# One float32 kernel of two transformer blocks: expert weights loaded by 2 MB into double places and by 1 MB into single ones

## The chip, the core and the metric

The kernel runs on one core of a Trainium2 chip. The metric is the device time of one execution in microseconds. Engines are called as the profile calls them: PE (matmuls), DVE (VectorE), ACT (ScalarE), POOL (GpSimd) and SP, whose queue issues most transfers.

## What is computed

Two blocks follow each other on 256 tokens of width 1024, in float32. The first has two layers, each with a gated feed-forward part, a mixer of attention and Fourier branches, and another feed-forward part. The second has one layer: a mixer of block attention and gated linear attention, and a mixture of 32 experts of which every token takes four. Cut to the part that matters here:

```python
logits = tokens @ w_router + b_router
top_logits, top_idx = lax.top_k(logits, 4)
top_w = softmax(top_logits)
def expert(e, rows):                      # the tokens that chose e
    hid = tokens[rows] @ w_exp_in[e] + b_exp_in[e]       # [n, 1024] @ [1024, 2048]
    return clamped_swiglu(hid) @ w_exp_out[e] + b_exp_out[e]   # [n, 1024] @ [1024, 1024]
y = sum over the chosen experts of top_w * expert
out = rmsnorm(x + gate2 * y, final_norm_w)
```

## The kernel before

All weights come as one stream of chunks, class `Stream` (lines 253 to 331). A chunk is one transfer of usually 1 MB, [128, 2048] float32. `load` (line 264) takes the first of a ring of places, `self.raw`, and issues the transfer on SP's queue (line 272). `convert` (line 278) takes half a chunk, a piece, and makes the two parts whose sum is the weight: `wh` on ACT (line 284) and `wl`, the rest, on DVE (line 285). When the second piece of a chunk is converted, its place is free and `load` is called again. `get` (line 319) hands out the next piece to the matmuls; before it does, `fill` converts until five pieces are ahead. In the program's order the conversion is therefore up to five pieces, HL, ahead of the matmuls. All engines work through their instructions in the order in which this Python code emits them, and SP's queue likewise: a load that has to wait for its place holds up the loads behind it.

The ring has three places of its own (RAW). At the end of the second mixer `more` (line 292, called in lines 1260 and 1279) adds four places in tiles of the second mixer that are free by then (pool `p2`, tags `r0` to `r3`), for good, and two in the tiles of the transposed input (`xth`, `xtl`) which serve once.

The expert stage, `moe`, runs over quarters q: `hidden(e, j)` takes a quarter of the first layer of expert e, q = 4 e + j, two chunks of 1 MB, and multiplies it with the slots of the expert's tokens (lines 1536 and 1537, one matmul with `wh` and one with `wl` for each of eight blocks of the contraction). `outputs(e, j)` does the same with a quarter of the second layer, one chunk of 1 MB (lines 1579 and 1580); it runs five quarters behind. So the stream of the stage, written out in the loop ahead of line 390, is: two first-layer chunks of quarter q, then (from q = 5) one second-layer chunk of quarter q - 5. Between them stand the smaller steps: the activation on DVE and ACT (`folded`, lines 1549 to 1565), the copies out of the accumulators (lines 1539 and 1584), the sum over the experts (line 1523), and for each group of four experts the gathering of its tokens (lines 1475 and 1493). `later` defers such a step by a number of pieces.

The loop over q at the end of `moe` also places some steps by hand. At q = 17, 20 and 22 come the transposition of the expert weights and the sum of the second-layer biases (`bias_part`, `bias_sum`, line 1597). At q = 26 the pool `bp`, which holds the biases, is left, and the last two rows, the gate of the residual and the gain of the last norm, each spread over all partitions, are loaded in its place as `fin` on POOL's queue (line 1631). `gated_sum` (lines 1607 and 1608) is the first to use them, after the last expert.

Of the kernel before, what the change touches and what calls it, by code (L numbers as in the profile page):

```python
# [23 lines left out]
OUT_ORDER = [*range(4 * NE - 3), 4 * NE - 2, 4 * NE - 3, 4 * NE - 1]  # L24
GLA_LEVELS = [1, 2, 4, 8, 16, 32, 64]


# ---------------------------------------------------------------- weight stream
# [77 lines left out]
# ---------------------------------------------------------------- constants of the shapes  # L106
# [47 lines left out]
# ---------------------------------------------------------------- data layout on the host  # L154
def cols(v):
    """[..., 128 n] -> [128, ..., n]: a vector as columns of 128."""
    v = np.asarray(v)
    return np.ascontiguousarray(np.moveaxis(v.reshape(*v.shape[:-1], -1, 128), -1, 0))


def layout(a):
    o = {}
    parts = []
    for ch in dense_chunks():
# [5 lines left out]
        a["w_exp_in_2"][0].reshape(NE, 2, 4, 128, 4, 256, 2).transpose(0, 4, 1, 3, 2, 6, 5)  # L170
    ).reshape(NE, 4, 2, 128, 2048)
# [29 lines left out]
# ---------------------------------------------------------------- the program  # L201
def build(tc, I, out):
# [26 lines left out]
    # persistent  # L229
# [22 lines left out]
    # ------------------------------------------------ weight stream  # L252
    class Stream:
        """Weight chunks: loaded whole, split into two exact float32r parts by halves, and given out by halves."""

        def __init__(self, chunks, raw, hl):
            self.ch, self.raw, self.hl = chunks, [(raw, "raw")] * RAW, [hl] * HL
            self.d = self.c = self.u = self.step = 0
            self.R, self.C = {}, {}
            self.pre, self.post = [], []  # L260
            self.side = self.units = None
            self.hold = False

        def load(self, parts=1):
            if self.d < len(self.ch):
                ap, w = self.ch[self.d]
                p, tag = self.raw[0]
                self.raw = self.raw[1:] + self.raw[:1]
                r = p.tile([128, 2048], FT, name="raw", tag=tag)
                for i in range(parts):  # L270
                    sl = slice(w // parts * i, w // parts * (i + 1))
                    SP.dma_start(r[:, sl], ap[:, sl])
                    if parts == 2 and i == 0:
                        load_x(256, 512)
                self.R[self.d] = r
                self.d += 1

        def convert(self):
            i, h = divmod(self.c, 2)
            r, w = self.R[i], self.ch[i][1] // 2  # L280
            p = self.hl[self.c % len(self.hl)]
            hi = p.tile([128, 1024], FR, name="wh")
            lo = p.tile([128, 1024], FR, name="wl")
            A.activation(hi[:, :w], r[:, h * w:h * w + w], AF.Copy)  # L284
            V.tensor_tensor(lo[:, :w], r[:, h * w:h * w + w], hi[:, :w], OP.subtract)  # L285
            self.C[self.c] = (hi, lo)
            self.c += 1
            if h:
                del self.R[i]
                self.load()  # L290

        def more(self, p, tags, once=False):
            """Further places for raw chunks, filled at once and, unless once, again in their turn."""
            for tag in tags:
                self.raw.insert(0, (p, tag))
                self.load()
                if once:
                    self.raw.pop()
# [10 lines left out]
        def start(self):  # L309
            self.load(2)  # L310
            load_x(512, D)
            for _ in range(RAW - 1):
                self.load()

        def fill(self):
            while self.c < min(self.u + len(self.hl), 2 * len(self.ch)):
                self.convert()

        def get(self):
            self.step += 1  # L320
# [4 lines left out]
            if self.u % 2 == 0:  # L325
                if self.units:
                    self.units.step()
# [23 lines left out]
    def mm_tok(ps, X, klist, w, last, mid=None):  # L351
        """ps[t] += X[k]^T W[k] for the k of a chunk; mid comes between the chunk's halves."""
# [11 lines left out]
    def wide(p, X, lo=0, hi=8):  # L364
        """p [128 outputs, 256 tokens] += W[k]^T X[k] for the k of half a chunk."""
# [5 lines left out]
    def rms_power(o, ss, scale, eps):  # L371
        """o = (ss * scale + eps) ** -0.5"""
# [17 lines left out]
    raw = enter("raw", RAW)  # L390
    hl = enter("hl", HL)
    st = Stream(dense, raw, hl)
# [21 lines left out]
    # ---------------------------------------- side work of the first block, a piece per chunk  # L414
# [72 lines left out]
    def make_xt(X, src, half, gcol=None, after=None):  # L487
        """X[k] = (src columns k)^T * gcol for the four k of a half."""
# [17 lines left out]
    def rms_of(ss, eps, name="rstd", pre=None):  # L506
        """(mean + eps) ** -0.5 from the halves' sums of squares, which pre scales first."""
# [8 lines left out]
    class Norm:  # L516
        """The normed, transposed x of the next stage, in two halves of the columns."""
# [18 lines left out]
    # ---------------------------------------- FFN  # L536
# [74 lines left out]
    # ---------------------------------------- units of softmax work, stepped between chunks  # L611
    class Steps:
        """Units under way take one stage per chunk, the oldest first; one new unit starts per chunk."""
# [12 lines left out]
        def finish(self):  # L626
            while self.step():
                pass
            st.units = None

    # ---------------------------------------- first mixer
    def mixer(l, norm, next_gain):
# [16 lines left out]
        # -- Fourier branch between the projections  # L649
# [17 lines left out]
        def row_rstd(dg):  # L667
            """rstd along the free dimension, on every partition"""
# [61 lines left out]
        # -- attention, in steps between the chunks of the values and the gates  # L730
# [53 lines left out]
        def diff_unit(h, qt):  # L784
# [39 lines left out]
            # the heads' norms; their gain comes with the transposition  # L824
# [18 lines left out]
        st.units = att  # L843
# [29 lines left out]
        # -- branch outputs, gated and merged  # L873
# [36 lines left out]
        # -- output projection  # L910
# [881 lines left out]
```

## Time and profile before

| | us |
|---|---|
| three runs, median (lowest to highest) | 2688.63 (2688.14 to 2689.32) |
| profiled execution, its span | 2688.0 |
| PE busy | 2605.0 |
| DVE busy | 2080.7 |
| ACT busy | 1723.2 |

The profiled execution has no time of its own beside its span; the span runs from its first instruction to its last and lies 0.6 us under the median of the runs. Busy times are unions of an engine's instructions over the span. The expert stage takes the part from about 1622 us to the end; what lies before it belongs to the first block and the second mixer. A group of instructions is read as: line, engine, operation, output and inputs, count, busy time, mean duration in ns, idle time of the engine just before them and what ended most of it.

### The profile page before, as it was taken

The page shows a single profiled execution, that of the slowest core. Times are in us where ns is not written, and L with a number is a line of the kernel's source. Part 1 is how long each engine was busy: PE and PEld are TensorE (multiplying, and loading weights), DVE is VectorE, ACT ScalarE, POOL GpSimd, SP SyncE. Part 2 cuts the span into 40 slices and gives each one's busy share as a digit, 9 for nine tenths or more (in the row PEclk, how much of TensorE's full clock was granted, in tenths as well). Part 3 has the DMA queues.
Part 4 walks back from the last instruction along what each step waited for, and adds up shares of the span by engine and source line. Part 5 has one row for each costly group of instructions (what it writes and reads, how often), then busy time and mean ns, then how long its engine had stood idle before and what let it go on. Part 6 is the DMA issues. An engine that isn't in the chain of part 4 may idle for free.

```text
span 2688.0 us, 34842 instructions
## 1 busy us (share of the span) xinstructions
PE 2605.0 (97%) x12700; PEld 2092.6 (78%) x12700; DVE 2080.7 (77%) x2717; ACT 1723.2 (64%) x2290; POOL 182.6 (7%) x255
## 2 busy tenths in 40 slices
PE   8999999999999999999999998999999999999996
PEld 6889888887787978778798886777777777777775
DVE  5656766666666676655656679999999999999997
ACT  5444554444444454544555538989898989888886
POOL 1000000001101000000000102000000000000000
PEclk9999999999999999999999999999999999999999
DMA  7655445655566444565444566999999999999995
GB/s 282 220 216 207 153 149 192 221 218 211 213 225 245 149 153 172 193 226 180 158 149 151 175 246 251 381 399 389 381 393 388 386 388 391 388 393 389 390 395 203
DMA packets 106227, 712.89 MB, mean 265 GB/s; under 512 B 13380, under 2 KB 14052, under 8 KB 25409
## 3 DMA queue, kind: packets, MB, share of 16 engines
q1 hardware_dynamic: 92976, 667.03, 65.9%
q0 software_dynamic: 12928, 43.05, 4.3%
q8 instruction: 101, 1.65, 0.2%
q14 instruction: 78, 0.63, 0.1%
q10 hardware_dynamic: 144, 0.52, 0.0%
HBM read 709.40 MB, written 3.77 MB: 265 GB/s over the span
## 4 chain that ended last, share of the span: by engine, by line
PE 84%; DVE 9%; issue 3%; ACT 3%; DMA 0%; POOL 0%; DVEq 0%; SPq 0%; ACTq 0%; POOLq 0%
PE hid L1536 7%; PE hid L1537 6%; DVE wl L285 6%; PE po L1580 3%; PE pf L1549 3%; PE g L347 3%; PE u L347 3%; PE g L348 3%; PE u L349 3%; PE g L349 3%; PE u L348 3%; PE d L347 3%; PE d L349 3%; PE d L348 3%; PE y L1523 3%
## 5 line engine op out<-in xcount | busy, mean ns | idle before, releaser
L285 DVE TENSOR_TENSOR wl<-raw,wh 128x1024 fp32r<-128x1024 f32 (+2 forms) x1274 | 1504.7, 1218 | 424.7 <-ACT wh L284 414.9
L284 ACT ACTIVATE wh<-raw 128x1024 fp32r<-128x1024 f32 (+2 forms) x1274 | 1294.3, 1050 | 527.7 <-PE d L349 126.5
L1536 PE MATMUL hid<-wh,xgt 128*128 128x512 f32 x1024 | 441.0, 431 | 0.2 <-ACT hs L1539 0.2
L1537 PE MATMUL hid<-wl,xgt 128*128 128x512 f32 x1024 | 404.8, 395 | 0.0
L1580 PE MATMUL po<-wl,act 128*128 128x512 f32 x512 | 208.6, 407 | 32.9 <-DVE wl L285 32.9
L1536 PEld LDWEIGHTS hid<-wh,xgt 128*128 128x128 f32 x1024 | 193.3, 189 | 54.3 <-issue 16.1
L1537 PEld LDWEIGHTS hid<-wl,xgt 128*128 128x128 f32 x1024 | 193.3, 189 | 53.3 <-issue 14.3
L1579 PE MATMUL po<-wh,act 128*128 128x512 f32 x512 | 204.0, 398 | 2.8 <-ACT osb L1584 2.8
L1580 PEld LDWEIGHTS po<-wl,act 128*128 128x128 f32 x512 | 96.1, 188 | 78.5 <-DVE wl L285 57.6
L347 PE MATMUL g<-wh,xth 128*128 128x512 f32 (+1 forms) x384 | 147.0, 383 | 0.0
L347 PE MATMUL u<-wh,xth 128*128 128x512 f32 (+1 forms) x384 | 146.0, 380 | 0.0
L348 PE MATMUL g<-wl,xth 128*128 128x512 f32 (+1 forms) x384 | 144.8, 377 | 0.0
L349 PE MATMUL g<-wh,xtl 128*128 128x512 f32 (+1 forms) x384 | 144.5, 376 | 0.0
L349 PE MATMUL u<-wh,xtl 128*128 128x512 f32 (+1 forms) x384 | 144.4, 376 | 0.0
L348 PE MATMUL u<-wl,xth 128*128 128x512 f32 (+1 forms) x384 | 144.1, 375 | 0.0
L347 PE MATMUL d<-wh,hth 128*128 128x512 f32 x352 | 139.8, 397 | 0.0
L349 PE MATMUL d<-wh,htl 128*128 128x512 f32 x352 | 138.8, 394 | 0.0
L348 PE MATMUL d<-wl,hth 128*128 128x512 f32 x352 | 138.8, 394 | 0.0
L1549 PEld LDWEIGHTS pf<-fold,hs 128*128 128x128 f32 x1024 | 130.8, 192 | 8.8 <-issue 1.3
L1549 PE MATMUL pf<-fold,hs 128*128 128x64 f32 x1024 | 129.1, 269 | 1.4 <-DVE v L1555 0.9
L1523 PE MATMUL y<-osb,ohw 128*128 128x512 f32 x256 | 123.0, 603 | 2.1 <-ACT osb L1584 2.1
L1493 POOL TENSOR_TENSOR wdup<-oh,wgt 128x128 f32<-128x128 f32 x64 | 72.5, 1162 | 741.4 <-PE wts L1500 510.0
(488 smaller groups left out, 4441.6 us busy)
## 6 DMA issues: line engine op xcount, KB each, us to landing
raw<-d_exp_in SPq DMA_DIRECT2D x256, 1024.0 KB, 7.3
raw<-d_dense SPq DMA_DIRECT2D x245, 1024.0 KB, 4.8
raw<-d_exp_out SPq DMA_DIRECT2D x128, 1024.0 KB, 7.5
ada_w<-d_ada POOLq DMA_DIRECT2D x96, 256.0 KB, 4.6
bias<-tables POOLq DMA_DIRECT2D x2, 1920.0 KB, 12.7
bg<-d_b_gate POOLq DMA_DIRECT2D x12, 256.0 KB, 4.2
raw<-d_dense SPq DMA_DIRECT2D x4, 768.0 KB, 4.5
raw<-d_dense SPq DMA_DIRECT2D x5, 512.0 KB, 3.6
```

The costliest lines, as they stand in the source:

```text
L284: A.activation(hi[:, :w], r[:, h * w:h * w + w], AF.Copy)
L285: V.tensor_tensor(lo[:, :w], r[:, h * w:h * w + w], hi[:, :w], OP.subtract)
L347: T.matmul(ps, lhsT=xh, rhs=wh, start=start, stop=False)
L348: T.matmul(ps, lhsT=xh, rhs=wl, start=False, stop=False)
L349: T.matmul(ps, lhsT=xl, rhs=wh, start=False, stop=stop_)
L1493: G.tensor_tensor(d[:, :, c], oh, wg, OP.mult)
L1523: T.matmul(y[t][n], lhsT=grp[e // 4].w[:, e % 4, t], rhs=osb[e, n], start=e == 0, stop=e == NE - 1)
L1536: T.matmul(ph, lhsT=lhs, rhs=wh[:, 512 * i:512 * i + 512], start=k == 0, stop=False)
L1537: T.matmul(ph, lhsT=lhs, rhs=wl[:, 512 * i:512 * i + 512], start=False, stop=k == 7)
L1549: T.matmul(pf[:, 4 * (c // 2) + 2 * (j % 2) + c % 2], lhsT=hs[:, 128 * c:128 * c + 128], rhs=fold, start=True, stop=True)
L1579: T.matmul(po, lhsT=lhs, rhs=wh[:, 512 * i:512 * i + 512], start=k == 0, stop=False)
L1580: T.matmul(po, lhsT=lhs, rhs=wl[:, 512 * i:512 * i + 512], start=False, stop=k == 7)
```

## The change

The first layer of an expert is stored and loaded by quarters of 2 MB, [128, 4096], which are converted in four pieces of the same size as before. The stream has two kinds of places. A double place holds 2 MB, a single one 1 MB. The three own places are one tile now; while dense weights are loaded they are three single places. When no dense chunk is left to load, places 0 and 1, once converted, are held back and become one double place, and place 2 goes on as the only single one. The tiles of `p2` become two double places (`r23`, `r01`), the transposed input's tile one double place that serves once. At q = 14 the pool `bp` is left and a further single place, `hx`, takes its memory. When no first-layer load is left, double places serve as single ones. Of the chunks of both sizes that have a free place, the one that comes first in the stream is loaded first.

The two parts of a piece share a tile, and so do pairs of tiles in the second mixer and of the transposed input. The bias steps come at q = 8, 10 and 12. The last two rows are loaded after the last first-layer quarter, on SP's queue, into a single place. The constants KIND_IN and KIND_OUT set every expert chunk to HALVES, conversion by pieces of 1024 columns; the other two kinds, WHOLE and DIRECT, are not used. Cut to its core:

```diff
+KIND_IN, KIND_OUT = HALVES, (HALVES, HALVES, HALVES, HALVES)
...
-        a["w_exp_in_2"][0].reshape(NE, 2, 4, 128, 4, 256, 2).transpose(0, 4, 1, 3, 2, 6, 5)
-    ).reshape(NE, 4, 2, 128, 2048)
+        a["w_exp_in_2"][0].reshape(NE, 2, 4, 128, 4, 256, 2).transpose(0, 4, 3, 1, 2, 6, 5)
+    ).reshape(NE, 4, 128, 4096)
...
+            self.todo = {w: [i for i, (_, n) in enumerate(chunks) if (n > 2048) == (w > 2048)] for w in (2048, 4096)}
+            self.own = raw.tile([128, 2048 * RAW], FT, name="raw")
+            self.free, self.held = {2048: list(range(RAW)), 4096: []}, []
...
+        def place(self, w):
+            p = self.free[w].pop(0)
+            if isinstance(p, int):
+                return p, self.own[:, 2048 * p:2048 * p + w]
+            pool_, tag = p
+            return p, pool_.tile([128, w], FT, name="raw", tag=tag)
+        def load(self, parts=1, most=1000):
+            for _ in range(most):
+                ready = [w for w in (2048, 4096) if self.free[w] and self.todo[w]]
+                if not ready:
+                    break
+                w = min(ready, key=lambda w: self.todo[w][0])
+                i = self.todo[w].pop(0)
+                self.T[i], r = self.place(w)
...
+                    SP.dma_start(r[:, sl], ap[:, sl])
...
+            if not self.todo[4096]:
+                self.free[2048] += self.free[4096]
+                self.free[4096] = []
+        def done(self, i):
+            del self.R[i]
+            p = self.T.pop(i)
+            if p not in self.once:
+                w = 4096 if self.ch[i][1] > 2048 else 2048
+                if w == 2048 and p in (0, 1) and self.todo[2048] and self.todo[2048][0] >= DENSE:
+                    self.held.append(p)
+                    if len(self.held) == 2:
+                        self.free[4096].append(0)
+                else:
+                    self.free[w].append(p)
+                self.load()
...
+                    both = self.part("w")
+                    hi, lo = both[:, :1024], both[:, 1024:]
...
+        def rows(self, srcs):
+            _, r = self.place(2048)
+            for i, src in enumerate(srcs):
+                SP.dma_start(r[:, 1024 * i:1024 * i + 1024], src)
+            return r[:, :1024], r[:, 1024:]
...
-            dense += [(I["exp_in"][q // 4, q % 4, h], 2048) for h in range(2)]
+            dense.append((I["exp_in"][q // 4, q % 4], 4096))
...
     def new_xt():
-        return (xtp[0].tile([128, 8, S], FR, name="xth"), xtp[0].tile([128, 8, S], FR, name="xtl"))
+        t = xtp[0].tile([128, 2, 8, S], FR, name="xt")
+        return t[:, 0], t[:, 1]
...
-        st.more(p2, ("r2", "r3", "r0", "r1"))
+        st.more(p2, ("r23", "r01"), 4096)
...
-        st.more(xtp[0], ("xth", "xtl"), once=True)
+        st.more(xtp[0], ("xt",), 4096, once=True)
...
-            if q == 17:
+            if q == 8:
                 later(POST, 1, bias_part)
-            if q in (20, 22):
-                later(POST, 1, lambda: bias_sum(q // 2 - 10))
+            if q in (10, 12):
+                later(POST, 1, lambda: bias_sum(q // 2 - 5))
...
-            if q == 26:
+            if q == 14:
                 leave("bp")
-                fp = enter("fin", 1, side="right")
-                for src in (bcast_row(mods, D, 3 * D), bcast_row(I["final_norm"], D)):
-                    fin.append(fp.tile([128, D], FT, name=f"fin{len(fin)}"))
-                    G.dma_start(fin[-1], src)
+                st.more(enter("hx", 1, side="right"), ("hx",), 2048)
+            if q == 4 * NE:
+                fin.extend(st.rows((bcast_row(mods, D, 3 * D), bcast_row(I["final_norm"], D))))
```

## Rows read from the trace of the kernel before

**Rows 1.** The page: the span, and each engine's busy time, share and instructions.

```profile
span 2688.0 us, 34842 instructions
PE 2605.0 (97%) x12700; PEld 2092.6 (78%) x12700; DVE 2080.7 (77%) x2717; ACT 1723.2 (64%) x2290; POOL 182.6 (7%) x255
```

**Rows 2.** Busy times by window, expert stage; last columns: granted clock, DMA share, GB/s.

```profile
1740.00:1900.00 160.00, 156.00 (x715) 118.67 (x715) 158.13 (x180) 142.44 (x179) 10.53 (x10) 1.00 0.99 392
1900.00:2100.00 200.00, 192.91 (x903) 149.38 (x903) 197.13 (x225) 177.83 (x226) 11.18 (x12) 0.99 0.99 386
...
2500.00:2640.00 140.00, 133.61 (x609) 101.11 (x608) 139.32 (x157) 123.90 (x153) 5.78 (x4) 1.00 0.99 394
sum 900.00, PE 868.26 PEld 666.23 DVE 890.74 ACT 802.90 POOL 52.91; mean PE 173.65 PEld 133.25 DVE 178.15 ACT 160.58 POOL 10.58
```

**Rows 3.** Groups by line and shape, window 1760 to 2600 us.

```profile
L285 DVE TENSOR_TENSOR wl<-raw,wh 128x1024 fp32r<-128x1024 f32 x621 | 722.4, 1220 | 5.3 <-ACT wh L284 1.3
L284 ACT ACTIVATE wh<-raw 128x1024 fp32r<-128x1024 f32 x621 | 620.3, 1051 | 7.0 <-PE hid L1536 6.3
...
L1537 PE MATMUL hid<-wl,xgt 128*128 128x512 f32 x828 | 327.1, 395 | 0.0
L1580 PE MATMUL po<-wl,act 128*128 128x512 f32 x416 | 169.7, 408 | 27.5 <-DVE wl L285 27.5
...
L1597 PE MATMUL y<-bo,wgtT 32*128 32x512 f32 x8 | 4.0, 613 | 0.0
```

**Rows 4.** Waits in that window (engine, line, released by: total, times, longest); SP's queue first.

```profile
SPq L272 <- DVE wl L285: 605.4, 253, 4.5
...
POOL fin L1631 <- PE y L1597: 63.8, 1, 63.8
...
DVE wl L285 <- ACT wh L284: 1.3, 3, 0.5
```

**Rows 5.** Transfers in that window: GB/s in 40 slices of 21 us; issues, median to landing.

```profile
GB/s 415 379 418 371 404 387 394 379 361 404 382 389 396 382 377 397 384 399 391 389 368 402 396 386 386 404 376 379 399 394 380 404 373 394 383 401 388 385 396 409
...
raw<-d_exp_in SPq DMA_DIRECT2D x208, 1024.0 KB, 7.3
raw<-d_exp_out SPq DMA_DIRECT2D x103, 1024.0 KB, 7.5
```

**Rows 6.** Line 272's time to landing: 1760 to 2600 us, then 0 to 1560 us (dense).

```profile
DMA to landing us min/median/max: 5.8/7.4/9.1
...
DMA to landing us min/median/max: 3.2/4.8/12.0
```

**Rows 7.** SP's queue in time order, 1695 to 1720 us: start, duration, issue.

```profile
1695.58 2.60 SPq L272 DMA_DIRECT2D raw<-d_exp_in  x2
1700.12 0.33 SPq L272 DMA_DIRECT2D raw<-d_exp_out  x1
1703.99 2.60 SPq L272 DMA_DIRECT2D raw<-d_exp_in  x2
1708.86 0.33 SPq L272 DMA_DIRECT2D raw<-d_exp_out  x1
```

**Rows 8.** DVE in time order, the end of the kernel.

```profile
2650.52 5.76 DVE L285 TENSOR_TENSOR wl<-raw,wh 128x1024 fp32r<-128x1024 f32 x5
...
2664.89 1.22 DVE L285 TENSOR_TENSOR wl<-raw,wh 128x1024 fp32r<-128x1024 f32 x1 [0.28 <-ACT wh L284]
2671.42 0.69 DVE L1607 TENSOR_TENSOR osb<-y,fin 128x512 f32<-128x512 f32 x1 [5.31 <-PE y L1523]
```

**Rows 9.** The transfers of the last two rows: size, median time to landing.

```profile
fin<-mods POOLq DMA_DIRECT2D x1, 512.0 KB, 7.6
fin<-d_final_norm POOLq DMA_DIRECT2D x1, 512.0 KB, 10.7
```

**Rows 10.** Busy times by window around the start of the experts (columns as in Rows 2).

```profile
1620.00:1630.00 10.00, 8.14 (x42) 7.59 (x42) 8.83 (x13) 8.32 (x13) 1.70 (x2) 0.66 0.23 79
1650.00:1660.00 10.00, 8.43 (x48) 6.76 (x48) 9.93 (x14) 9.52 (x14) 8.47 (x7) 1.00 0.43 163
```

More of the change, by code (lines that the diff above doesn't have):

```diff
@@ L260, in __init__, with pieces @@
             self.pre, self.post = [], []
-            self.side = self.units = None
+            self.side = self.steps = None
+            self.T, self.once = {}, set()
             self.hold = False
[L264 to L271, printed above, removed]
+        def pieces(self, i):
+            return 4 if self.ch[i][1] > 2048 else 2
@@ new lines, in place @@
+        def place(self, w):
[12 more added lines that the diff above has]
+                self.T[i], r = self.place(w)
+                ap, n = self.ch[i]
+                for k in range(parts):
+                    sl = slice(n // parts * k, n // parts * (k + 1))
@@ L292, in more @@
[L292 to L298, printed above, removed]
+                self.R[i] = r
+            if not self.todo[4096]:
[13 more added lines that the diff above has]
+                self.load()
@@ new lines, in part @@
+        def part(self, name):
+            p, tag = self.hl.pop(0)
+            self.hl.append((p, tag))
+            return p.tile([128, 2048], FR, name=name, tag=tag)
+        def convert(self):
+            i, h, kind = self.units[self.c]
+            r, w = self.R[i], self.ch[i][1]
+            if kind == DIRECT:
+                self.C[self.c] = (r, None)
+            else:
+                if kind == HALVES:
+                    w //= self.pieces(i)
+                    both = self.part("w")
+                    hi, lo = both[:, :1024], both[:, 1024:]
+                else:
+                    hi, lo = self.part("wh"), self.part("wl")
+                r = r[:, h * w:h * w + w]
+                A.activation(hi[:, :w], r, AF.Copy)
+                V.tensor_tensor(lo[:, :w], r, hi[:, :w], OP.subtract)
+                self.C[self.c] = (hi, lo)
+            self.c += 1
+            if kind == WHOLE or kind == HALVES and h == self.pieces(i) - 1:
+                self.done(i)
@@ L300, in due, with more @@
+        def more(self, p, tags, w, once=False):
+            for tag in tags:
+                if once:
+                    self.once.add((p, tag))
+                self.free[w].insert(0, (p, tag))
+                self.load()
+        def rows(self, srcs):
[3 more added lines that the diff above has]
+            return r[:, :1024], r[:, 1024:]
         def due(self, q):
@@ L309, in start, with parts @@
         def start(self):
-            self.load(2)
+            self.load(2, 1)
             load_x(512, D)
-            for _ in range(RAW - 1):
-                self.load()
+            self.load()
         def fill(self):
-            while self.c < min(self.u + len(self.hl), 2 * len(self.ch)):
+            def parts(n):
+                return {HALVES: 1, WHOLE: 2, DIRECT: 0}[self.units[n][2]]
+            while self.c < len(self.units) and \
+                    sum(parts(n) for n in range(self.u, self.c + 1)) <= len(self.hl):
+                if self.units[self.c][0] not in self.R:
+                    break
                 self.convert()
         def get(self):
-            self.step += 1
+            if self.u and self.units[self.u - 1][2] == DIRECT:
+                self.done(self.units[self.u - 1][0])
+            self.step += 1 if self.units[self.u][2] == HALVES else 2
             self.due(self.pre)
@@ L388, in build @@
             dense.append((I["exp_out"][e, j // 2, j % 2], 2048))
-    raw = enter("raw", RAW)
-    hl = enter("hl", HL)
-    st = Stream(dense, raw, hl)
+    raw = enter("raw", 1)
+    hl = enter("hl", 1)
+    DENSE = len(dense_chunks())
+    kinds = [HALVES] * DENSE
+    for q in range(4 * NE + 5):
+        kinds += [KIND_IN] * (q < 4 * NE)
+        kinds += [KIND_OUT[OUT_ORDER[q - 5] % 4]] * (q >= 5)
+    st = Stream(dense, kinds, raw, hl)
     sm = enter("small", 2)
@@ L628, in finish @@
                 pass
-            st.units = None
+            st.steps = None
     def mixer(l, norm, next_gain):
@@ L1201, in gla_unit @@
             A.activation(junk[:, :256], ob[:, t, vs], AF.Square, accum_out=obs[:, 4 * t + h:4 * t + h + 1])
-        att = st.units = Steps([gla_unit(h, t) for h in range(4) for t in range(2)])
+        att = st.steps = Steps([gla_unit(h, t) for h in range(4) for t in range(2)])
         zb = enter("zb", 2)
@@ L1523, in combine, with weigh @@
             T.matmul(y[t][n], lhsT=grp[e // 4].w[:, e % 4, t], rhs=osb[e, n], start=e == 0, stop=e == NE - 1)
+        unit = {}
+        def weigh(ps, x, k, start, stop_):
+            n = k % 4
+            if n == 0 or n == 2 and unit["kind"] == HALVES:
+                unit["kind"] = st.units[st.u][2]
+                unit["w"] = get()
+            wh, wl = unit["w"]
+            if unit["kind"] == HALVES:
+                n %= 2
+            sl = slice(512 * n, 512 * n + 512)
+            x = x.rearrange("p c s -> p (c s)")
+            if unit["kind"] == DIRECT:
+                T.matmul(ps, lhsT=x.bitcast(FT), rhs=wh[:, sl], start=start, stop=stop_)
+            else:
+                T.matmul(ps, lhsT=x, rhs=wh[:, sl], start=start, stop=False)
+                T.matmul(ps, lhsT=x, rhs=wl[:, sl], start=False, stop=stop_)
         def hidden(e, j):
@@ L1528, in hidden @@
             ph = hbank("hid")
[L1529 to L1537 removed]
+            for k in range(8):
+                if e + j == 0 and k in (2, 4):
+                    grp[0].pair(k + 2)
+                weigh(ph, X[k // 4][:, k % 4, e % 4], k, k == 0, k == 7)
             hs = w2.tile([128, 512], FT, name="hs")
@@ L1573, in outputs @@
             po = pos_[n]
[L1574 to L1580 removed]
+            for k in range(4 * kh, 4 * kh + 4):
+                weigh(po, act[e][:, k], k, k == 0, k == 7)
             if kh:
@@ L1722, in rest @@
                 for h in range(2):
-                    w = weights(I["exp_in"][one, j, h])
+                    w = weights(I["exp_in"][one, j, :, 2048 * h:2048 * h + 2048])
                     for i in range(4):
```

62 lines of the change are left out of this document (20 added, 42 removed).

## The prediction

> **What bounds the kernel now.** The profiled execution has a span of 2688.0 us [rows 1]; the runs shown have a median of 2688.63 us, 0.6 us more, so a sum made against the span is moved over to the median unchanged. I read the page first. PE is busy for 97% of the span and would be named the bound by that figure alone [rows 1]. The change touches the expert stage, so next come the busy times by window over that stage, 1740 to 2640 us [rows 2]: VectorE (DVE) is busy 890.7 of 900 us, PE 868.3, ScalarE (ACT) 802.9, and the DMA engines show a share of 0.99 at 386 to 394 GB/s. Three resources look full, so the waits must decide. The groups of instructions by line say that DVE's subtraction `wl` (line 285) takes 1220 ns and sat idle before it for 5.3 us in 840, while PE waited 27.5 us at line 1580 for exactly that subtraction [rows 3]. The list of waits has no line in which ACT or DVE waits for a weight transfer; the transfers are what waits: SP's queue stood 605.4 us for DVE to free a place [rows 4]. So **DVE sets the pace**, and the stream keeps up with it. How closely it keeps up is the question here.
>
> One quarter of an expert (index q, 128 of them) reads 2 MB of first-layer and 1 MB of second-layer weights. In the stretch of 840 us 208 first-layer transfers were issued, two per quarter [rows 5], so a quarter lasts 840/104 = 8.08 us.
>
> **The change, part by part.**
>
> *Places.* Before, 1 MB transfers go in order round seven places. A transfer is on its way for 7.4 us (5.8 to 9.1) in this stage [rows 6], out of 7 x 2.69 = 18.9 us that a place is held; the data lie ready long before DVE wants them. After, the first layer has three double places (the fourth, in the transposed-input tile, serves once), so the load of quarter q+3 goes out when quarter q has been converted: 24 us for 2 MB, ample. The second layer is different. Places 0 and 1 become the third double place when the dense weights end, so the second layer has **one place**, number 2, until the place `hx` is opened at q = 14. It holds the first second-layer chunk (used at q = 5) from early on. The nine that follow, used at q = 6 to 14, can each be issued only when the chunk before has been converted, and are wanted one quarter later. The tenth goes into `hx`, after which two places give each load a quarter more, and the wait ends.
>
> *What one of the nine costs.* SP issues in order on one queue, and second-layer loads leave 2.3 to 2.6 us after the last first-layer load [rows 7]; after the change the 2 MB load of quarter q+3 stands just ahead. Neither a 2 MB load nor one behind it is in the trace, so I bound it. The best slice moved 418 GB/s [rows 5], 1.049 MB in 2.51 us; a 1 MB transfer without a full queue lands after 4.8 us [rows 6], so 2.3 us are not movement. The last of 3 MB lands 2.3 + 3 x 2.51 = 9.8 us after the issue of the first-layer load. It should be there when DVE has finished the next quarter's first layer, 8.08 us after that issue, less the 1.05 us that ACT's `wh` needs ahead of DVE [rows 3]: 7.0 us. That leaves 2.8 us of stall. But a stall falls after the issue of the next first-layer load, so that load gains what was lost: successive stalls add up to 2.8 us in pairs, **1.4 us per quarter** at the low end. For the high end I take the stage's slowest rate, 386 GB/s [rows 2], hence 2.72 us per MB, and add the spread of landings, 9.1 - 7.4 = 1.7 us, because a late transfer is lost and an early one gives nothing back: 2.3 + 8.15 + 1.7 = 12.2 us, a stall of 5.2 us, 2.6 per quarter. Between them I take **2.0 us**, the middle, as the queue will be emptier than in the rows of before but landings will still scatter. DVE has no slack to make it up later [rows 2]. Nine quarters: 9 x 2.0 = **18 us**, ends 12.6 and 23.4, and 25 if each of the nine lost the whole 2.8.
>
> The Trainium skill (DMA: Bandwidth & Descriptors, Anatomy of one DMA) fits one transfer as about 2.0 us plus its bytes at 436 GB/s, for the software-generated path. By that fit the last of 3 MB would land after 9.2 us, the stall would be 1.1 us per quarter, and the sum about 10 us, where the rows give 12.6 at the least; here the rows decide. The Trainium skill (Trainium Kernel Development and Optimization, Best Practices) asks to double-buffer so that DMA and compute overlap, which speaks against a single place; no row of before shows a stream with one.
>
> *The start.* Nine places are filled before the experts begin, with 9 MB either way: at 1620 to 1630 us the DMA engines move only 79 GB/s, since nothing is free [rows 10]. After the change one of the nine holds a second-layer chunk early, and the first-layer loads behind it have 5 quarters' time. 0 us.
>
> *Longer rows.* A first-layer transfer moves 16 KB per partition instead of 8. No row shows that; the two rates used above, 418 and 386 GB/s, stand for a better and a worse one.
>
> *Steady state from q = 15.* DVE's work is the same six conversions per quarter at the same width, so 8.08 us stays: 0 us, covered by DVE itself. Half as many first-layer issues (128 fewer SP instructions) save nothing, as SP mostly waits [rows 4].
>
> *Joined tiles.* The two parts of a converted piece, of `xt` and of the second mixer's tiles now share a tile, so a writer waits for the last reader of both halves. In `prod` the readers of the two halves end one matmul apart, 0.4 us by the nearest row [rows 3]. For some ten new `xt` tiles that is 0 to 4 us; nothing here removes work, so no gain. I take 0.5 us. In the experts ACT may be released one matmul later, but DVE waited only 1.3 us for ACT [rows 4]: 0.
>
> *The bias steps* move from q = 17 to 22 to q = 8 to 12. They are eight matmuls of about 0.6 us, 4.0 us in all [rows 3], with transposes and one ACT copy; DVE has no part in them. Cost 0 under DVE's work, 4 us if that cover were gone. POOL's queue loses two DMA issues that waited 63.8 us for these matmuls with nobody waiting for them [rows 4]: 0.
>
> *The last rows.* Two transfers of 512 KB move from POOL to the end of SP's queue. They go into `hx` when the chunk four before the last has been converted. Ten conversions belong to the last five chunks. The row at 2650.52 us merges five conversions and six more follow, the last at 2664.89, so the second of the ten is the third of that row and ends at about 2654 us [rows 8]. With the slowest landing of these rows in the busy stage, 10.7 us [rows 9], they are there at 2665, and the first use is at 2671.4 [rows 8]. Cost 0, with 6 us of cover; the bound if it failed is the same 10.7 us.
>
> Sum: 2688.6 + 18 + 0.5 = **2707 us**.
>
> **The rivals.**
>
> *No stall of size (within 0.2%).* If second-layer loads land within about 7.6 us of the first-layer issue, the nine stalls stay under 0.6 us each. For it: in the busy stage a load lands in as little as 5.8 us [rows 6]. Against: that row is for 1 MB, and 2 MB more stand ahead. The time would be about 2691 us.
>
> *DMA is the bound and longer transfers relieve it (faster).* For it: the share of 0.99. Against: nobody waits for a weight. It could at most give back DVE's idle time in the stage, 900 - 890.7 = 9.3 us [rows 2], by way of the gaps before line 285: 2679 us. It decides only if the slowed stretch from q = 6 to 14 costs less than that. The fit on the skill's page named above would have two 1 MB transfers cost 2.0 us more than one of 2 MB. The trace moves a MB every 2.69 us, well under one transfer's time, so fixed parts overlap and are not paid.
>
> *The second place comes late, or a loaded stream stays short with two (much slower).* Every further quarter costs another 2.0 us: ten more give 2727 us, all of them some 2930. For it: `hx` takes memory that other tiles leave. Against: the old `fin` tiles took the same memory, and their load left as soon as the bias matmuls ended [rows 4]. A second form: PE, waiting more, is granted a lower clock, as at 1620 to 1630 us (0.66). But at 1650 to 1660 it was busy only 84% of the time and kept 1.00 [rows 10].
>
> **How the numbers follow.** A measurement of this kernel can tell about 0.2%, 5.4 us, from no change: faster is below 2683.2, slower above 2694.0. The forecast has a chance of 0.76, the first rival 0.13, the second 0.05, the third 0.06. Hence faster 0.05, same 0.13, slower 0.82. The forecast's own ends are 2701 (12.6 us) and 2714 (25 us). The range is 2692 to 2717: down into the first rival's reach, and up by the 3.5 us that the joined tiles may cost beyond what is taken.
>
> **What would show it.** Right: in the changed profile, a stretch of about 75 us near 1660 to 1745 us in which DVE's busy share drops to some 80%, ACT's `wh` waits for transfers into `raw`, and second-layer issues come one per 10 us; after it the pace is 8.08 us again and DVE 99% busy. Half the first-layer issues, each 2 MB. `fin` waits for nobody at the end. Wrong: that stretch is as full as before, DVE idles on throughout the stage, or the time lies under 2694 us.

## The result and the profile after

The changed kernel takes **2710.3 us** (median of four runs, 2708.95 to 2713.3), the kernel before 2688.39 us in four runs of the same comparison. The ratio is 1.0079, with a 95% interval of [1.0066, 1.0092]. The change costs 21.9 us, and the profiled executions show nearly the same: their spans are 2709.0 and 2688.0 us, 21.0 us apart. In the program of after, the two parts of a piece come from ACT in line 335 (`w<-raw`) and from DVE in line 336; every load of the stream is issued in line 295.

The first view is the page: span, busy times, and the expert loads with their size and median time to landing.

```profile
span 2709.0 us, 34061 instructions
PE 2615.1 (97%) x12700; PEld 2096.4 (77%) x12700; DVE 2080.0 (77%) x2717; ACT 1722.5 (64%) x2290; POOL 180.0 (7%) x253
...
raw<-d_exp_in SPq DMA_DIRECT2D x128, 2048.0 KB, 9.5
...
raw<-d_exp_out SPq DMA_DIRECT2D x128, 1024.0 KB, 8.6
```

DVE has done the same work as before: 2080.0 us in 2717 instructions, against 2080.7 [rows 1]. So the 21 us of added span are idle time, and the question is where that lies. The busy times by window over the expert stage answer it (columns as in [rows 2]):

```profile
1660.00:1760.00 100.00, 86.35 (x376) 63.35 (x375) 78.57 (x89) 70.94 (x91) 7.01 (x6) 0.95 0.83 312
1760.00:1860.00 100.00, 96.04 (x450) 73.97 (x450) 98.98 (x114) 88.80 (x114) 2.69 (x4) 1.00 0.98 384
1860.00:2060.00 200.00, 193.06 (x899) 147.93 (x898) 198.24 (x225) 179.22 (x225) 14.26 (x12) 1.00 0.98 390
...
2460.00:2660.00 200.00, 193.22 (x891) 147.73 (x890) 197.51 (x224) 177.81 (x222) 5.80 (x4) 1.00 0.98 387
```

The first of these stretches in the kernel before:

```profile
1660.00:1760.00 100.00, 96.71 (x458) 74.83 (x457) 99.06 (x113) 89.77 (x115) 7.36 (x6) 1.00 0.96 375
```

DVE is busy 78.57 us of the first 100, where it was busy 99.06. That is 20.5 us lost in one stretch. From 1760 us on it is as full as before. Even the DMA engines fell there, from a share of 0.96 at 375 GB/s to 0.83 at 312: they too had nothing to do for part of the time, because the next load had no place. Ahead of the stretch nothing is lost. DVE's step for the second quarter of the experts starts at the same time in both kernels:

```profile
1656.60 0.68 DVE L1643 TENSOR_TENSOR v<-pf,ebias 128x512 f32<-128x512 f32 x1
```

```profile
1656.49 0.69 DVE L1555 TENSOR_TENSOR v<-pf,ebias 128x512 f32<-128x512 f32 x1
```

The first line is of after, the second of before: 0.11 us apart. Now the waits of after, from 1660 to 1780 us (engine and line, what released it: total, times, longest):

```profile
ACT w L335 <- DMA raw<-d_exp_out: 22.3, 9, 4.7
DVE w L336 <- ACT w L335: 21.3, 12, 4.2
...
PE po L1616 <- DVE w L336: 9.4, 10, 1.5
```

**Nine** waits for second-layer transfers, 22.3 us together, 2.5 each. ACT waits for the transfer, DVE for ACT, PE for DVE. No such line is in [rows 4], nor in after from 1780 us on. The single waits stand in ACT's timeline (start, duration, idle time before and its releaser):

```profile
1671.09 2.95 ACT L335 ACTIVATE w<-raw 128x1024 fp32r<-128x1024 f32 x3 [4.66 <-DMA raw<-d_exp_out]
...
1680.90 2.96 ACT L335 ACTIVATE w<-raw 128x1024 fp32r<-128x1024 f32 x3 [0.75 <-DMA raw<-d_exp_out]
...
1691.42 1.06 ACT L335 ACTIVATE w<-raw 128x1024 fp32r<-128x1024 f32 x1 [2.37 <-DMA raw<-d_exp_out]
...
1701.29 3.90 ACT L335 ACTIVATE w<-raw 128x1024 fp32r<-128x1024 f32 x4 [0.79 <-DMA raw<-d_exp_out]
...
1711.73 2.96 ACT L335 ACTIVATE w<-raw 128x1024 fp32r<-128x1024 f32 x3 [3.68 <-DMA raw<-d_exp_out]
...
1721.74 3.90 ACT L335 ACTIVATE w<-raw 128x1024 fp32r<-128x1024 f32 x4 [0.93 <-DMA raw<-d_exp_out]
...
1732.75 2.95 ACT L335 ACTIVATE w<-raw 128x1024 fp32r<-128x1024 f32 x3 [4.25 <-DMA raw<-d_exp_out]
...
1742.65 3.91 ACT L335 ACTIVATE w<-raw 128x1024 fp32r<-128x1024 f32 x4 [1.31 <-DMA raw<-d_exp_out]
...
1753.02 2.95 ACT L335 ACTIVATE w<-raw 128x1024 fp32r<-128x1024 f32 x3 [3.60 <-DMA raw<-d_exp_out]
```

SP's queue in time order, for three of these quarters:

```profile
1681.03 0.33 SPq L295 DMA_DIRECT2D raw<-d_exp_in  x1
1684.72 0.33 SPq L295 DMA_DIRECT2D raw<-d_exp_out  x1
1690.04 0.33 SPq L295 DMA_DIRECT2D raw<-d_exp_in  x1
1696.50 0.33 SPq L295 DMA_DIRECT2D raw<-d_exp_out  x1
1701.37 0.33 SPq L295 DMA_DIRECT2D raw<-d_exp_in  x1
1705.10 0.33 SPq L295 DMA_DIRECT2D raw<-d_exp_out  x1
```

Two kinds of quarter alternate. In the **long** one the second-layer load leaves close behind a 2 MB load (1681.03, then 1684.72) and is there at 1691.42, 10.4 us after the first-layer issue. ACT was ready 2.37 us earlier. In the **short** one the stall before has let the first-layer load go ahead (1690.04), and the second-layer load leaves alone, at 1696.50. It still takes 4.79 us, and ACT was ready at 1701.29 - 0.79 = 1700.50, 4.00 us after the issue. So a short stall of 0.8 us remains even where the head start works. Of the 22.3 us, the five long waits make up 18.6 and the four short ones 3.8. Issues of the second layer are 11.8 and 8.6 us apart (1684.72, 1696.50, 1705.10), a sum of 20.4 us for a pair of quarters that took 16.2 before.

### The profile page after: what moved, and what is told of

The parts are those of the page before. It is cut to its first block, busy times and chain, and to the rows that moved or that the text cites. A ratio compares the mean times of both kernels' runs of the same rounds, so it can differ in the third digit from the quotient of the medians.

```text
span 2709.0 us, 34061 instructions
## 1 busy us (share of the span) xinstructions
PE 2615.1 (97%) x12700; PEld 2096.4 (77%) x12700; DVE 2080.0 (77%) x2717; ACT 1722.5 (64%) x2290; POOL 180.0 (7%) x253
## 4 chain that ended last, share of the span: by engine, by line
PE 69%; DVE 23%; issue 4%; DMA 2%; ACT 1%; POOL 0%; DVEq 0%; ACTq 0%; SPq 0%; POOLq 0%
DVE w L336 17%; PE u L411 3%; PE g L411 3%; PE g L412 3%; PE g L413 3%; PE u L413 3%; PE u L412 3%; PE d L411 3%; PE d L412 3%; PE d L413 3%; PE z L411 3%; PE z L412 2%; PE z L413 2%; PE hid L1615 2%; PE hid L1616 2%
## 5 line engine op out<-in xcount | busy, mean ns | idle before, releaser
L336 DVE TENSOR_TENSOR w<-raw,w 128x1024 fp32r<-128x1024 f32 (+2 forms) x1274 | 1504.5, 1217 | 448.2 <-ACT w L335 440.4
L335 ACT ACTIVATE w<-raw 128x1024 fp32r<-128x1024 f32 (+2 forms) x1274 | 1299.0, 1050 | 568.7 <-PE u L413 127.2
L1615 PE MATMUL hid<-w,xgt 128*128 128x512 f32 x1024 | 440.9, 431 | 0.2 <-ACT hs L1627 0.2
L1616 PE MATMUL hid<-w,xgt 128*128 128x512 f32 x1024 | 404.8, 395 | 0.1
L1616 PE MATMUL po<-w,act 128*128 128x512 f32 x512 | 211.7, 413 | 41.6 <-DVE w L336 41.5
L1615 PEld LDWEIGHTS hid<-w,xgt 128*128 128x128 f32 x1024 | 193.2, 189 | 54.3 <-issue 16.1
L1616 PEld LDWEIGHTS hid<-w,xgt 128*128 128x128 f32 x1024 | 193.1, 189 | 53.9 <-issue 14.6
L1615 PE MATMUL po<-w,act 128*128 128x512 f32 x512 | 206.4, 403 | 7.4 <-ACT w L335 4.6
L1616 PEld LDWEIGHTS po<-w,act 128*128 128x128 f32 x512 | 97.2, 190 | 90.6 <-DVE w L336 69.8
L411 PE MATMUL g<-w,xt 128*128 128x512 f32 (+1 forms) x384 | 147.3, 384 | 0.6 <-ACT w L335 0.6
L412 PE MATMUL g<-w,xt 128*128 128x512 f32 (+1 forms) x384 | 145.5, 379 | 0.5 <-DVE w L336 0.5
L411 PE MATMUL u<-w,xt 128*128 128x512 f32 (+1 forms) x384 | 145.9, 380 | 0.0
L413 PE MATMUL g<-w,xt 128*128 128x512 f32 (+1 forms) x384 | 144.8, 377 | 0.0
L412 PE MATMUL u<-w,xt 128*128 128x512 f32 (+1 forms) x384 | 144.4, 376 | 0.0
L413 PE MATMUL u<-w,xt 128*128 128x512 f32 (+1 forms) x384 | 144.3, 376 | 0.0
L411 PE MATMUL d<-w,hth 128*128 128x512 f32 x352 | 139.8, 397 | 0.0
L413 PE MATMUL d<-w,htl 128*128 128x512 f32 x352 | 138.8, 394 | 0.0
L412 PE MATMUL d<-w,hth 128*128 128x512 f32 x352 | 138.8, 394 | 0.0
```

The source lines that it names most:

```text
L335: A.activation(hi[:, :w], r, AF.Copy)
L336: V.tensor_tensor(lo[:, :w], r, hi[:, :w], OP.subtract)
L411: T.matmul(ps, lhsT=xh, rhs=wh, start=start, stop=False)
L412: T.matmul(ps, lhsT=xh, rhs=wl, start=False, stop=False)
L413: T.matmul(ps, lhsT=xl, rhs=wh, start=False, stop=stop_)
L1615: T.matmul(ps, lhsT=x, rhs=wh[:, sl], start=start, stop=False)
```

## The experiments

The theory: the loss is one second-layer place for nine quarters and nothing else. Its rivals: the 2 MB size of the first-layer transfers, the order in the queue alone, or some of the other edits (bias steps, shared tiles, last rows). The runs came in two groups of four; the kernel before had a median of 2689.42 us beside runs 1 to 4 and of 2689.69 us beside runs 5 to 8. Runs 4 and 7 were timed once, so they bear differences of tens of us only; the others were timed 4 to 11 times.

**1. A second place nine quarters earlier.** The bias steps, which hold the memory of `hx`, come at q = 2 to 4 and start the sum over the experts, so that `hx` opens at q = 5.

```diff
-            T.matmul(y[t][n], lhsT=grp[e // 4].w[:, e % 4, t], rhs=osb[e, n], start=e == 0, stop=e == NE - 1)
+            T.matmul(y[t][n], lhsT=grp[e // 4].w[:, e % 4, t], rhs=osb[e, n], start=False, stop=e == NE - 1)
...
-                T.matmul(y[t][n], lhsT=router.wT[:, t], rhs=router.bo[:, 512 * n:512 * n + 512], start=False, stop=False)
+                T.matmul(y[t][n], lhsT=router.wT[:, t], rhs=router.bo[:, 512 * n:512 * n + 512], start=True, stop=False)
...
-            if q == 8:
+            if q == 2:
                 later(POST, 1, bias_part)
-            if q in (10, 12):
-                later(POST, 1, lambda: bias_sum(q // 2 - 5))
+            if q in (3, 4):
+                later(POST, 1, lambda: bias_sum(q - 3))
...
-            if q == 14:
+            if q == 5:
                 leave("bp")
```

> The second single place opens at q = 5 instead of q = 14 (the bias steps come at q = 2 to 4 and start the sums instead of joining them, so that its memory is free). Theory (one single place is the whole loss): the nine stalls are gone, time 2688 to 2692 us, DVE over 98% busy from 1660 to 1760 us, no wait of ACT for a second-layer transfer. Rival (2 MB transfers and double places cost by their size, or the joined tiles do): the time stays at 2705 to 2712 us.

Measured: 2697.05 us, ratio 1.0027 [1.0017, 1.0037]. Some two thirds of the loss are gone, but the time is above the expected one. In its list of waits, ACT waits for the second layer once. ACT's timeline and SP's queue say why:

```profile
1672.08 2.95 ACT L335 ACTIVATE w<-raw 128x1024 fp32r<-128x1024 f32 x3 [4.97 <-DMA raw<-d_exp_out]
```

```profile
1660.28 0.33 SPq L295 DMA_DIRECT2D raw<-d_exp_in  x1
1660.83 2.45 SPq L295 DMA_DIRECT2D raw<-d_exp_out  x2
```

Of nine waits one is left, the first. `hx` opened so late that its first load left only at 1660.83, behind a 2 MB load (1660.28). One quarter earlier should do; that is run 5. The execution that was traced is the fastest of nine, 2694.13 us, 4.7 us over the kernel before, and this wait covers it. The other 2.9 us up to the median were not traced.

**2. Only the order of the queue.** With one single place still, a double place that comes free is refilled only after the next second-layer load has been issued, as long as there is one single place (q = 5 to 14).

```diff
...
+                elif w == 4096 and self.single:
+                    self.late.append(p)
                 else:
                     self.free[w].append(p)
                 self.load()
+                if w == 2048 and self.late:
+                    self.free[4096] += self.late
+                    self.late = []
+                    self.load()
...
+            if q == 5:
+                st.single = True
             if q == 14:
+                st.single = False
```

> Still one single place until q = 14, but while there is one, a freed double place is refilled only after the next second-layer load has gone out. Theory (the second-layer load stands behind 2 MB in the queue): a second-layer load then lands in about 4.8 to 5.5 us, against 4.6 us that are free, so each of the nine stalls is under 1 us and the time is 2690 to 2697 us. Rival (one place is short whatever the order): the time stays at 2706 to 2712 us.

Measured: 2702.71 us, ratio 1.0048 [1.0031, 1.0065]: about 8 of 22 us come back. That lies between the two expectations and meets neither. The waits, SP's queue and ACT's timeline (ACT's line is 342 here):

```profile
ACT w L342 <- DMA raw<-d_exp_out: 14.4, 9, 4.9
```

```profile
1684.76 0.33 SPq L296 DMA_DIRECT2D raw<-d_exp_out  x1
```

```profile
1689.50 1.07 ACT L342 ACTIVATE w<-raw 128x1024 fp32r<-128x1024 f32 x1 [0.80 <-DMA raw<-d_exp_out]
```

The load stands ahead of the 2 MB load and is there after 4.74 us, but ACT was ready 3.94 us after the issue. In this run a single place leaves 3.0 to 4.0 us from its release to the next need, where the expectation had 4.6, and the loads that stand ahead of the 2 MB take 4.7 to 4.9 us. The first wait, 4.9 us, is as long as in the change: its load left at 1662.39 behind a 2 MB load of 1659.71, which the edit did not yet hold back. So queueing behind 2 MB is only one part of the loss; the lone place is short without it.

**3. The size alone.** The same places, but each 2 MB load issued as two of 1 MB.

```diff
-                for k in range(parts):
-                    sl = slice(n // parts * k, n // parts * (k + 1))
+                cut = 2 if n > 2048 else parts
+                for k in range(cut):
+                    sl = slice(n // cut * k, n // cut * (k + 1))
```

> The same places, each first-layer quarter loaded by two transfers of 1 MB in a row. Theory (places and order in the queue decide, not the size of a transfer): 2709 to 2713 us, as the changed kernel. Rival (the size of 2 MB itself costs): back towards 2690 us. Rival (the size of 2 MB saves something that hides in the loss): 2716 us and more.

Measured: 2709.59 us, ratio 1.0071 [1.0054, 1.0088]; the change itself has 1.0079 [1.0066, 1.0092]. ACT's nine waits are there as well:

```profile
ACT w L336 <- DMA raw<-d_exp_out: 23.5, 9, 5.3
```

The rival that the size of 2 MB makes the loss falls. A smaller cost or gain of the size, of a few us, would not show between these two intervals.

**4. The second place later.** `hx` opens at q = 22 instead of 14.

```diff
-            if q == 14:
+            if q == 22:
                 leave("bp")
```

> The second single place opens at q = 22 instead of q = 14, eight quarters later. Theory: eight more stalls of 2.2 to 2.5 us each, 2728 to 2731 us. Rival (the loss is a single event around the start of the second layer or the opening of the place): 2709 to 2713 us.

Measured: 2731.32 us in one run, 21.0 us over the change for eight more quarters with one place: 2.6 us each. ACT's waits for the second layer, from 1640 to 2000 us, are 17 now, eight more than nine:

```profile
ACT w L335 <- DMA raw<-d_exp_out: 42.9, 17, 5.0
```

The loss follows the place's opening.

**5. The second place one quarter earlier still.** Everything of run 1 one quarter earlier, with the weights of the first group of experts at q = 1 and 2: bias steps at q = 1 to 3, `hx` at q = 4.

```diff
-            if q == 2:
+            if q == 1:
                 later(POST, 1, bias_part)
-            if q in (3, 4):
-                later(POST, 1, lambda: bias_sum(q - 3))
+            if q in (2, 3):
+                later(POST, 1, lambda: bias_sum(q - 2))
...
-            if q == 5:
+            if q == 4:
                 leave("bp")
...
-            if q in (2, 3):
+            if q in (1, 2):
                 grp[0].step()
```

> The second single place opens one quarter earlier still, at q = 4 (bias steps at q = 1 to 3, the first group's weights at q = 1 and 2). In the run with q = 5 one wait of 5.0 us was left: the second chunk of the second layer went out only just behind the 2 MB of quarter 8. Theory: that wait goes too, 2688 to 2692 us. Rival (the rest of some 5 to 7 us is the price of 2 MB or of double places): 2694 to 2698 us.

Measured: 2692.04 us, ratio 1.0006 [0.9997, 1.0015], against 2689.69 us of before: at the upper end of what the theory expected. Its windows:

```profile
1660.00:1760.00 100.00, 96.40 (x462) 75.17 (x461) 98.98 (x115) 90.04 (x116) 6.80 (x5) 1.00 0.98 389
```

DVE is at 98.98 where after had 78.57 and before 99.06, and the list of waits of 1640 to 1780 us has no transfer in it. With two places from the first use on, the loss is gone, as far as the interval can tell. All other edits of the change are still in this kernel (2 MB loads, shared tiles, early bias steps, last rows on SP), so the interval bounds their sum, with that of the steps moved in this run, to between -0.8 and 4.0 us.

**6. Places divided the other way.** The three own places stay single until q = 14; only then do two of them become the third double place.

```diff
...
-                if w == 2048 and p in (0, 1) and self.todo[2048] and self.todo[2048][0] >= DENSE:
+                if self.pair and w == 2048 and p in (0, 1) and self.todo[2048] and self.todo[2048][0] >= DENSE:
...
             if q == 14:
+                st.pair = True
                 leave("bp")
```

> The other way to share out the same memory: until q = 14 the three own places all stay single ones, and only then two of them become the third double place; bias steps and the new place as in the changed kernel. Theory (a stream of loads needs two places, whichever stream it is): with two double and three single places the second layer never waits, and a first-layer load goes out 9 us before it is wanted against 7.2 us for 2 MB alone, so few and short waits, 2690 to 2696 us. Rival (three double places are needed): waits of ACT for first-layer transfers of over 1 us per quarter, 2698 us and more.

Measured: 2696.48 us, ratio 1.0024 [1.0014, 1.0033], 0.5 us above what the theory expected and below the rival. No wait for the second layer is left in that stretch; now ACT waits for the first:

```profile
ACT w L336 <- DMA raw<-d_exp_in: 6.3, 4, 4.2
```

The same nine MB, with three single places instead of one, cost 6.3 us of waits instead of 22.3. (The 7.2 us that the theory gives a 2 MB load by itself are too few: none in after landed in less than 7.5.) Which stream is short depends on the division, and the second layer had been given too little.

**7. The second place much later.** `hx` opens at q = 46.

```diff
-            if q == 14:
+            if q == 46:
                 leave("bp")
```

> The second single place opens at q = 46, 32 quarters later than in the changed kernel. Theory: every quarter with a single place costs the same, about 2.4 us, so 2785 to 2792 us. Rival (the wait wears off after some quarters): under 2770 us.

Measured: 2784.27 us in one run, 74 us over the change for 32 more quarters, 2.31 us each; just under the expected time, far from the rival. A window inside the longer stretch:

```profile
1860.00:2060.00 200.00, 173.97 (x707) 130.26 (x708) 157.74 (x179) 142.87 (x180) 5.07 (x8) 0.89 0.81 301
```

DVE is 79% busy here. In a long row of quarters the price is 2.3 us per use; the nine of the change cost 2.5 each, as the first one (4.66 us) is dearer than the rest (17.6 / 8 = 2.2). With 32 more quarters 41 waits were due, and the list from 1640 to 2150 us has 39:

```profile
ACT w L335 <- DMA raw<-d_exp_out: 86.9, 39, 5.4
```

Two more, of 2.1 and 3.0 us, it puts down to PE, although the load that ACT needed landed only 0.1 us before ACT went on (1795.55 and 1963.31). With them the waits are 92.0 us, of 94.6 us that the run takes over the kernel before.

**8. A version to beat both.** Run 5 with eight second-layer chunks multiplied as float32 without conversion. These eight of 128 chunks skip the two parts of ACT and DVE, which should free DVE of 16 subtractions.

```diff
-        kinds += [KIND_OUT[OUT_ORDER[q - 5] % 4]] * (q >= 5)
+        kinds += [DIRECT if q % 12 == 8 and 20 < q < 120 else KIND_OUT[OUT_ORDER[q - 5] % 4]] * (q >= 5)
```

> As e_q4, and eight second-layer chunks between q = 20 and q = 120 are not converted but multiplied as float32 straight from their place. DVE saves two conversions of 1.14 us in each, PE pays more for four float32 matmuls than for eight others. Theory (DVE sets the pace outside the stalls): about 8 x 2.3 = 18 us less than e_q4, 2670 to 2676 us. Rival (PE or the transfers hold the pace as closely as DVE): within 4 us of e_q4.

Measured: 2729.75 us, ratio 1.0146 [1.0131, 1.0162]: 38 us slower than run 5 instead of 16 to 22 faster, a plain miss. Run 8's waits and busy times from 1780 to 2600 us:

```profile
ACT w L335 <- PE hid L1616: 40.8, 85, 3.0
...
ACT w L335 <- DMA raw<-d_exp_out: 22.1, 11, 3.8
```

```profile
1780.00:2600.00 820.00, 782.71 (x3539) 595.28 (x3538) 766.03 (x873) 691.38 (x871) 46.03 (x48) 0.98 0.96 373
```

The same of run 5:

```profile
ACT w L335 <- PE hid L1616: 15.5, 77, 0.2
...
ACT w L335 <- DMA raw<-d_exp_out: 0.3, 1, 0.3
```

```profile
1780.00:2600.00 820.00, 788.90 (x3687) 607.10 (x3686) 812.47 (x925) 733.02 (x922) 50.88 (x48) 1.00 0.98 389
```

DVE has less to do and yet is idle for 54 us of 820 where it was idle for 7.5. Two waits of ACT have grown by much the same: those that the list puts down to second-layer transfers by 21.8 us, those that it puts down to PE by 25.3 us. A cause that fits the first: a chunk used directly holds its place until its last matmul, not only until its conversion five pieces ahead, and the second layer is back at one place meanwhile. PE's, SP's and ACT's timelines around one such chunk:

```profile
1884.51 3.60 PE L1613 MATMUL po<-raw,act 128*128 128x512 f32 x8
```

```profile
1877.96 0.33 SPq L295 DMA_DIRECT2D raw<-d_exp_out  x1
...
1889.06 3.64 SPq L295 DMA_DIRECT2D raw<-d_exp_out  x2
```

```profile
1900.07 2.96 ACT L335 ACTIVATE w<-raw 128x1024 fp32r<-128x1024 f32 x3 [3.02 <-PE hid L1616]
```

Its matmuls end at 1888.1, and the second layer's loads, of which a quarter of 8.1 us has one, leave none from 1877.96 to 1889.06. The load of 1889.06 landed at 1899.97, 0.1 us before ACT went on, so these 3.02 us are a wait for a transfer as well, though the list has them under PE. Chunks used directly come some 102 us apart, and all 11 waits that the list does put down to transfers end 2 to 18 us behind the first matmul of one. So that part, some 25 us, goes with these chunks, though no run varied how long they hold a place. Where ACT's added waits for PE come from, some 22 us, was not taken apart: for that half the cause of this miss stays open. No version that was run beats the kernel before; run 5 equals it within its interval.

## Why the prediction was right

The forecast was 2707 us in a range of 2692 to 2717, and 2710.3 us came, by the mechanism it named. Point by point:

- **DVE as the bound, no slack.** Right. Idle time of DVE and added span agree (20.5 us in the stretch, 21.0 in the span), nothing was made up later, and the pace after the stretch is that of before. From 1760 to 2600 us, 623 pieces in 840 us, where [rows 3] had 621:

```profile
L336 DVE TENSOR_TENSOR w<-raw,w 128x1024 fp32r<-128x1024 f32 x623 | 723.7, 1217 | 5.2 <-ACT w L335 1.2
L335 ACT ACTIVATE w<-raw 128x1024 fp32r<-128x1024 f32 x623 | 626.6, 1051 | 19.5 <-PE hid L1616 17.5 <-PE pf L1637 0.2
```

- **Nine stalls by one place.** Right in number, place and cause. Runs 4 and 7 moved the opening of `hx` alone, and the waits went with it, 17 and 41 where 9 + 8 and 9 + 32 are due; run 5 took them away; run 3 excluded the size as the cause.
- **The price of a stall.** The term was under-sized: 2.0 us taken, 18 in all; 22.3 / 9 = 2.5 us measured, near the high end of 2.6. The step that was mis-sized is the low end's sentence that the next load "gains what was lost", so that stalls "add up to 2.8 us in pairs". The head start is real, but the working asked only when the 2 MB load ahead leaves, not when the second-layer load's own place comes free. That load leaves 4.0 us before its need and takes 4.8 us by itself, so the second of a pair costs another 0.8 us or more. The pairs measured are 4.66 + 0.75, 2.37 + 0.79, 3.68 + 0.93 and 4.25 + 1.31 us, and a last long one of 3.60. The long ones, 3.7 us in the mean, lie inside the working's 2.8 to 5.2; the four short ones, 3.8 us in all, stood in it at nothing and make up most of the 4.3 us by which the term was short. Run 2 shows that lower limit with nothing ahead in the queue.
- **The landing behind 2 MB.** 10.4 us twice (from 1681.03 to 1691.42, from 1701.37 to 1711.73), inside the bounds of 9.8 and 12.2. The time available was put at 7.0 us; in these two it was 8.0 and 6.7 (the landing less the wait). That no load of about 2 MB is in the trace of before is not quite so: POOL's queue has two of 1920 KB, 12.7 us in the median, long before the experts. The Trainium skill (DMA: Bandwidth & Descriptors, Anatomy of one DMA) has a fit for the software-generated path; an estimate by it is 9.2 us here, and 4.4 us for 1 MB by itself. The trace is 1.2 us above the first, and has 4.7 to 4.9 us for the second.
- **Two places are enough.** Right, by run 5. The Trainium skill (Trainium Kernel Development and Optimization, Best Practices) asks for double-buffering. Run 5 agrees with it here: from nine waits to none in the stretch from 1640 to 1780 us.
- **Terms put at nothing.** The start: right, by the steps 0.11 us apart at 1656 us. The steady state: right, by the 623 pieces. Longer rows and bias steps: nothing seen, and run 5's interval bounds all the other edits together to 4.0 us. The 0.5 us for the joined tiles can't be told from 0. What they did show is ACT waiting longer for PE before it writes a piece, 17.5 us in these 840 where [rows 3] had 6.3; DVE's idle time did not grow (5.2 us, before 5.3), so this cost nothing. The last rows left SP at 2674.47 and 2674.85. In the list of transfers the second took 6.4 us, so they were there at 2681.3, 12 us before the first use, which waits for PE as before [rows 8]. The cover was larger than the 6 us worked out:

```profile
2674.47 0.33 SPq L354 DMA_DIRECT2D raw<-mods  x1
2674.85 0.42 SPq L354 DMA_DIRECT2D raw<-d_final_norm  x1
...
2693.49 0.69 DVE L1690 TENSOR_TENSOR osb<-y,raw 128x512 f32<-128x512 f32 x1 [5.08 <-PE y L1597]
```

- **The rivals.** "No stall of size" fell: the mean stall is 2.5 us. "DMA is the bound" fell: the time did not fall, and DVE's gaps before the subtraction are 5.2 us where before had 5.3, although the loads are twice as large. "The second place late" did not happen, but its price per quarter did come out when it was made to (2.3 to 2.6 us, where 2.0 was given). Its second form, the clock, is taken up at the end.

## What to carry to other kernels

When several streams share one in-order queue, count the places of each stream and write down, for each, the time from the release of a place to the need for what goes in next; it must exceed the landing time of that load by itself, and that of what stands ahead of it in the queue. A total that is the same (nine MB before and after) says nothing about it. Where a stream is short, try a second place for it first: here it gave back nearly all of the 22 us, the order of the queue about 8 and the size of the transfers nothing that could be told.

## What had not been expected of the hardware

In after from 1760 us on, a DMA share of 0.98 at 384 to 391 GB/s stands beside a stage in which no engine waits for a transfer; before had 0.99 at 386 to 394 [rows 2] and no such wait either. A 2 MB load takes 9.5 us in the median, a 1 MB load took 7.3 [rows 5], while the rate stays the same; from 1780 us on, where each stream has its places, the longer landing costs no wait.

PE's granted clock fell in the stalled stretch, to 0.95 in after with PE 86% busy, and to 0.89 in run 7 with 87%. With levels of 2.4 and 1.2 GHz these means are, as an estimate, a tenth and a fifth of the stretch at the lower one. The prediction had taken from a stretch with 84% and 1.00 [rows 10] that it would not. No run shows the cost of the clock by itself, and little is left for it: the waits for transfers are 22.3 us against a loss of 21.9 in after, and 92.0 us against 94.6 in run 7.
